# Splitting the transposed probabilities on GpSimd alone, and moving stores, loads and row sums in a hand-made order of attention heads

## The chip, the core and the metric

The kernel runs on one core of a Trainium2 chip. The core has five engines that run side by side, each through its own instructions in order: TensorE (PE in the profile; its weight loads are PEld), VectorE (DVE), ScalarE (ACT), GpSimd (POOL) and SyncE (SP), which here only starts transfers. Engines wait for each other through semaphores. The metric is the time of one execution on the device, in microseconds (us); lower is better.

## What is computed

The reference is a small decoder trunk on a sequence of 2048 tokens, width 1024, in float32: a Mamba-2 layer, then one layer of latent attention with 16 heads, then a last normalisation. Only the attention matters here. For each head, 128 queries at a time:

```python
s = s.astype(jnp.float32) * scale
mask = (q0 + local)[:, None] >= jnp.arange(kv_len)[None, :]
p = jax.nn.softmax(jnp.where(mask, s, -jnp.inf), axis=-1).astype(v.dtype)
outs.append(jnp.einsum('bhqk,bkhd->bqhd', p, v[:, :kv_len]))
```

The outputs of the heads are multiplied by a gate and by an output matrix and added to the residual.

## The kernel before

The program has three stages. The first (Mamba layer, projections, keys, values and queries written to DRAM) and the last (`back`: gate, output product, normalisation) are not touched. The middle stage, `attention` and its `heads`, is.

**Jobs.** `heads` works through 64 jobs `n`, one for each head `h` (16) and block `qb` of 512 queries (4 a head). Within a job, `j` counts four tiles of 128 queries, `c` counts blocks of 512 keys (`qb + 1` of them, the last cut to the causal width), and `k` counts tiles of 128 keys. Float32 accuracy is had from pairs of float16 numbers, a high and a low half, so every product is made two or three times.

**Steps.** Each step is a small function inside `heads` with a letter as its name:

- S, on TensorE: scores of one (j, c) into a PSUM bank (`mm3`, lines 279 to 281, three products, and the mask at line 1436).
- M, on VectorE: the negated maximum of each row of a bank (L1444). N, on VectorE: the row's shift from up to four maxima, with a constant added (L1449, or L1452 and L1453).
- E, on ScalarE: the exponential into a float32 tile `Pr` in SBUF, with the row's sum into `sum` (L1459). There are 20 `Pr` buffers. E gives the PSUM bank back.
- Key blocks other than c = 0, and all of `qb` 0, are turned on TensorE: T (L1481) transposes into PSUM, A on ScalarE (L1488) writes the high half and B on VectorE (L1493) the low half into `PTs`.
- The block c = 0 of the jobs with `qb` 1 to 3 (`TURNED`) is turned by DMA, 192 tiles in all: H on VectorE (L1465) casts `Pr` to float16, which is the high half in `HL`; L on GpSimd (L1469) subtracts it from `Pr`, which gives the low half and frees `Pr`; X on SyncE (L1475) starts a transposing DMA from `HL` to `PX`.
- V, on TensorE (L1507, L1508): the product with the values, `PTs` tiles first, `PX` tiles last in a job. F, on ScalarE (L1515): the job's output from PSUM to `Os`.
- O: two stores of `Os`. The first, on SyncE's queue (L1539), writes the product of the high halves of the values to `o_d` in DRAM. The second, on GpSimd's queue (L1540), adds the product of the low halves to the same place with an accumulating DMA, and so waits at GpSimd until the first has landed.
- R, on VectorE, once a head: row sums (L1520), reciprocal (L1521), a constant factor (L1522). Y, on TensorE (L1526), transposes them; Z (L1531, L1532) stores them.

**The order.** The stage is scheduled by hand. The class `Pace` plays the jobs through before the program is built: it books each step for a stated number of nanoseconds on its engine, with a stated delay until the next step may start, and appends the step to one list. The steps are then emitted in that list's order, and each engine runs its own in that order, however late the one at its head is. `queue(engine, rank, ...)` makes a step wait in the model until its engine is free; a lower rank goes first. A step that uses several engines, as O does, is appended once.

**Loads.** Queries, keys and values of the next head are loaded by SyncE. They are issued inside S of a job's first score (`load_q`, L1389 to L1391; for `qb` 2 also `load_k`, L1376 and L1377, and `load_v`, L1383), and the model of the order does not book them. The store O is appended when F ends in the model, without a booking either.

Of the kernel before, what the change touches and what calls it, by code (L numbers as in the profile page):

```python
# [15 lines left out]
AF = mybir.ActivationFunctionType  # L16
ALU = mybir.AluOpType
AX = mybir.AxisListType
# [3 lines left out]
P = 128  # L22
T = 2048
D = 1024
DI = 2048
G = 4
H = 32
NH = 16
EPS = 1e-6
TB = 512  # L30
NB = T // TB
# [16 lines left out]
def DVE(n):  # L48
    return 62 + n * 1.042, 135
KV2, CQ2, GA2, ALL2 = 0, 576, 1344, 3392  # L50
MAGIC = 12582912.0
PSCALE = 32768.0
PSHIFT = 10.397207708399179
# [18 lines left out]
class Pace:  # L72
# [79 lines left out]
    def scores(self, n, j, c):  # L152
        w, qb = self.width(n, j, c), self.jobs[n][1]
        self.give(ps=-1)
        self.scored += 1

        def maximum():
            self.issue("DVE", ("M", n, j, c), *DVE(w), after=counted)

        def counted():  # L160
            self.maxima[n, j] = self.maxima.get((n, j), 0) + 1
            if self.maxima[n, j] == qb + 1:
                self.queue("DVE", 1, lambda: self.issue("DVE", ("N", n, j), 100 if qb < 2 else 180, 110, shift))

        def shift():
            for x in range(qb + 1):
                self.queue("ACT", 2, lambda x=x: self.exp(n, j, x), lambda: self.free["Pr"] > 0)

        self.issue("PE", ("S", n, j, c), 3 * (w / 2.4 + 2.5) + 60 * (c == qb), 225,
                   lambda: self.queue("DVE", 2, maximum))  # L170

    def exp(self, n, j, c):
        w = self.width(n, j, c)
        self.give(Pr=-1)

        def done():
            self.give(ps=1)
            self.scored -= 1
            if (j, c) == (3, NB - 1):
                self.queue("DVE", 3, lambda: self.issue("DVE", ("R", n), 600, 130, summed))  # L180
            if c in self.turned[self.jobs[n][1]]:
                self.queue("DVE", 3, lambda: self.high(n, j, c),
                           lambda: self.free["HL"] > 0 and ((n, c) in self.dma or self.free["PX"] > 0))
            else:
                self.probs[n, j, c] = w // P

        def summed():
            self.sums.append(n)

        self.issue("ACT", ("E", n, j, c), 300 + w * 0.7, 40, done)  # L190

    def high(self, n, j, c):
        self.give(HL=-1, PX=-((n, c) not in self.dma))
        self.dma.setdefault((n, c), 4)

        def low():
            self.issue("POOL", ("L", n, j, c), 1364, 60, moved)

        def moved():
            self.give(Pr=1)  # L200
            self.queue("SP", 1, lambda: self.issue("SP", ("X", n, j, c), 1300, DMA_DELAY, landed))

        def landed():
            self.give(HL=1)
            self.dma[n, c] -= 1
            if not self.dma[n, c]:
                for k in range(4 * c, 4 * c + 4):
                    self.pairs[n, k] = "PX"

        self.issue("DVE", ("H", n, j, c), 345, 130, lambda: self.queue("POOL", 1, low))  # L210

    def rows(self, n):
        self.give(ps=-1)
# [24 lines left out]
    def values(self, n, k):  # L238
        w, qb = (4 - self.first(n, k)) * P, self.jobs[n][1]
        if n not in self.opened:  # L240
            self.opened[n] = 4 * qb + 4
            self.give(ps=-1)
        self.opened[n] -= 1
        last = not self.opened[n]

        def done():
            if self.pairs[n, k] == "PTs":
                self.give(PTs=1)
            else:
                c = k // 4  # L250
                self.dma[n, c] -= 1
                self.give(PX=self.dma[n, c] == -4)
            if last:
                self.queue("ACT", 0, lambda: self.issue("ACT", ("F", n), 495, 110, closed))

        def closed():
            self.order.append(("O", n))
            self.give(ps=1)

        self.issue("PE", ("V", n, k), 2 * (w / 2.4 + 2.5), 225, done)  # L260


class Net:
# [42 lines left out]
    def split(self, hi, lo, src, scale=None):  # L306
        nc = self.nc
        if scale is None:
            nc.scalar.activation(hi, src, AF.Copy)  # L309
            nc.vector.tensor_tensor(lo, src, hi.bitcast(F32), ALU.subtract)  # L310
        else:
            nc.scalar.activation(hi, src, AF.Copy, scale=scale)
            nc.vector.scalar_tensor_tensor(lo, src, scale, hi.bitcast(F32), ALU.mult, ALU.subtract)
# [1093 lines left out]
    def heads(self, sp):  # L1407
        nc, v = self.nc, self.nc.vector
        keys, vals, quer = self.keys, self.vals, self.quer
        pace = Pace(TURNED)  # L1410
        jobs = pace.jobs
        used = {"mm": 0, "tr": 0}
        sums, shifts, maxima, banks, probs, turned, halves, moved, outs = ({} for _ in range(9))

        def bank(first):
            tag = first if used[first] < 4 else "tr" if first == "mm" else "mm"
            used[tag] += 1
            return self.t(self.pp, tag, [P, TB], bufs=4), tag

        def S(n, j, c):  # L1420
            h, qb = jobs[n]
            if j == c == 0:
                if qb == 0:
                    sums[h] = self.t(sp, "sum", [P, 16, 4], bufs=3)
                    nc.gpsimd.memset(sums[h], 0.0)
                if h + 1 < NH:
                    if qb == 2:
                        self.load_k(h + 1, 0, NB, nc.sync)
                        self.load_v(h + 1, nc.sync)
                    self.load_q(h + 1, qb, nc.sync)  # L1430
            Q, K, w = quer[h, qb], keys[h], pace.width(n, j, c)
            s, tag = bank("mm")
            qs, ks = slice(j * P, (j + 1) * P), slice(c * TB, c * TB + w)
            self.mm3(s[:, :w], Q[:, 0, qs], Q[:, 1, qs], K[:, 0, ks], K[:, 1, ks], True, c < qb)
            if c == qb:
                nc.tensor.matmul(s[:, w - P:w], self.idb, self.mk, start=False, stop=True)
            if c == 0:
                shifts[n, j] = self.t(sp, "nm", [P, 1], bufs=4)
                maxima[n, j] = self.t(sp, "mx", [P, 4], bufs=4)
            banks[n, j, c] = s, tag, w  # L1440

        def M(n, j, c):
            s, _, w = banks[n, j, c]
            v.tensor_reduce(maxima[n, j][:, c:c + 1], s[:, :w], AX.X, ALU.max, negate=True)  # L1444

        def N(n, j):
            qb, m, nm = jobs[n][1], maxima.pop((n, j)), shifts[n, j]
            if qb == 1:
                v.tensor_scalar(nm, m[:, 0:1], m[:, 1:2], PSHIFT, ALU.min, ALU.add)  # L1449
                return  # L1450
            if qb:
                v.tensor_reduce(nm, m[:, :qb + 1], AX.X, ALU.min)  # L1452
            v.tensor_scalar(nm, nm if qb else m[:, 0:1], PSHIFT, None, ALU.add)  # L1453

        def E(n, j, c):
            h, qb = jobs[n]
# [3 lines left out]
                                 accum_out=sums[h][:, 4 * qb + j, c:c + 1])  # L1460
            used[tag] -= 1

        def H(n, j, c):
            u = halves[n, j, c] = self.t(sp, "HL", [P, 2, TB], F16, bufs=BUFS["HL"])
            v.tensor_copy(u[:, 0], probs[n, j, c])  # L1465

        def L(n, j, c):
            u = halves[n, j, c]
            nc.gpsimd.tensor_tensor(u[:, 1], probs.pop((n, j, c)), u[:, 0], ALU.subtract)  # L1469

        def X(n, j, c):
            if (n, c) not in moved:
# [38 lines left out]
        def F(n):  # L1511
            h, qb = jobs[n]
            o, tag, _ = outs[n]
            u = outs[n] = self.t(sp, "Os", [P, TB], bufs=3)
            nc.scalar.activation(u, o, AF.Copy)  # L1515
            used[tag] -= 1

        def R(n):
            ri = outs["ri"] = self.t(sp, "ri", [P, 16], bufs=2)
            v.tensor_reduce(ri, sums[jobs[n][0]], AX.X, ALU.add)  # L1520
            v.reciprocal(ri, ri)  # L1521
            v.tensor_scalar(ri, ri, 0.5 * PSCALE, None, ALU.mult)  # L1522

        def Y(n):
            outs["ps"] = bank("tr")
# [2 lines left out]
        def Z(n):  # L1528
            ps, tag = outs["ps"]
            r = self.t(sp, "rT", [16, P], bufs=2)  # L1530
            nc.scalar.activation(r, ps[:16, 0:P], AF.Copy)  # L1531
            nc.sync.dma_start(self.ri_d[jobs[n][0]].rearrange("(j q) -> j q", q=P), r)  # L1532
            used[tag] -= 1

        def O(n):
            h, qb = jobs[n]
            o = outs.pop(n)
            od = self.o_d[h * 64:(h + 1) * 64, qb * TB:(qb + 1) * TB]
            nc.sync.dma_start(od, o[0:64, :])  # L1539
            nc.gpsimd.dma_start(od, o[64:128, :], accum_op=ALU.add)  # L1540
            if h == NH - 3:
                self.load_wo(qb)

        steps = dict(S=S, M=M, N=N, E=E, H=H, L=L, X=X, T=T, A=A, B=B, V=V, F=F, O=O, R=R, Y=Y, Z=Z)
        for what, *where in pace.run():
            steps[what](*where)

# [197 lines left out]
```

## Time and profile before

| | us |
|---|---|
| median of 3 runs | 3231.45 |
| lowest and highest run | 3227.48, 3243.19 |
| profiled execution, its own time | 3242.9 |
| its span, first to last instruction | 3241.0 |
| attention stage in it (from the first score to the last output) | 2062 to 3055, 993 long |

A page of the profile gives, for each engine, the time in which it was busy and its share of the span; then the span in 40 slices, with the TensorE clock that was granted in tenths of full speed; then groups of instructions with their mean durations. Other views of the same trace answer questions for a stretch of time: who waited for whom, the instructions in order of time, and the busy time of each engine by window. Times within the trace are microseconds from the span's start. A wait is put down to the instruction that released it last, so an instruction just behind the true cause can stand there.

### The profile page before, as it was taken

Reading aid. Unit: us, or ns where it says so; the run is one execution under the profiler, and the core shown is the slowest. Engines: PE = TensorE matmul, PEld = TensorE weight load, DVE = VectorE, ACT = ScalarE, POOL = GpSimd, SP = SyncE. Lnnn points to the kernel's source line nnn. Section 1 sums busy time; section 2 is a strip of 40 time slices with the busy share of each in tenths; the row PEclk is TensorE's granted clock in tenths of the full one; section 3 lists DMA queues with packets and bytes.
Section 4 is the critical chain, followed back from the end, with each engine's and each line's share of the span. In section 5 each row is a group of like instructions: output and inputs, shape, how many; then the busy total and the mean of one; then the engine's idle time right before and its main releaser. Section 6 shows DMA issues by size and latency. Waiting matters only on the chain. (4 is left out here: it accounts for less than half of the span.)

```text
span 3241.0 us, 49983 instructions
## 1 busy us (share of the span) xinstructions
PE 3004.5 (93%) x17047; PEld 1876.4 (58%) x17047; DVE 2324.8 (72%) x4739; ACT 1882.4 (58%) x4760; POOL 699.0 (22%) x822
## 2 busy tenths in 40 slices
PE   8999999999999999999999999988888988887898
PEld 6777655555655556555655545455544554544687
DVE  6878887787777777877654454677877776888665
ACT  7878566666565565655434333566666666666422
POOL 1222112211212112112121122322322222224200
PEclk9999999999999999999999999999989999998999
DMA  5443666555554356544376566564565565565585
GB/s 174 130 127 122 203 225 223 187 179 172 196 184 147 114 178 223 182 146 149 120 252 205 162 195 189 138 113 88 104 118 93 98 121 95 95 131 125 116 269 173
DMA packets 456371, 507.11 MB, mean 156 GB/s; under 512 B 262626, under 2 KB 316130, under 8 KB 454676
## 3 DMA queue, kind: packets, MB, share of 16 engines
q1 hardware_dynamic: 439012, 457.37, 50.7%
q0 software_dynamic: 17104, 46.55, 5.2%
q8 instruction: 135, 2.21, 0.3%
q14 instruction: 120, 0.98, 0.1%
HBM read 332.21 MB, written 121.25 MB: 140 GB/s over the span
## 5 line engine op out<-in xcount | busy, mean ns | idle before, releaser
L1459 ACT ACTIVATE Pr<-mm,nm 128x512 f32<-128x512 f32 (+3 forms) x522 | 324.0, 629 | 95.2 <-POOL HL L1469 61.5
L1444 DVE TENSOR_REDUCE mx<-mm 128x1 f32<-128x512 f32 (+3 forms) x522 | 308.4, 602 | 72.7 <-PE mm L281 50.0
L1493 DVE TENSOR_TENSOR PTs<-tr,PTs 128x512 f16<-128x512 f32 (+2 forms) x447 | 251.8, 570 | 113.6 <-ACT PTs L1488 110.2
L279 PE MATMUL mm<-xT,wsp 128*128 128x512 f16 (+1 forms) x800 | 308.7, 386 | 0.8 <-ACT wsp L309 0.8
L280 PE MATMUL mm<-xT,wsp 128*128 128x512 f16 (+1 forms) x800 | 306.3, 383 | 0.0
L1469 POOL TENSOR_TENSOR HL<-Pr,HL 128x512 f16<-128x512 f32 x192 | 236.0, 1368 | 320.6 <-ACT Os L1515 123.3
L281 PE MATMUL mm<-xT,wsp 128*128 128x512 f16 (+1 forms) x800 | 304.6, 383 | 0.3 <-DVE wsp L310 0.2
L1488 ACT ACTIVATE PTs<-tr 128x512 f16<-128x512 f32 (+2 forms) x447 | 221.1, 509 | 139.1 <-PE tr L1481 136.8
L1481 PE MATMUL tr<-pack,Pr 128*128 128x128 f32 x1407 | 235.2, 288 | 32.7 <-ACT Pr L1459 16.7
L279 PE MATMUL mm<-K,xT 96*128 96x512 f16 (+4 forms) x530 | 192.8, 364 | 69.0 <-ACT Pr L1459 67.8
L279 PE MATMUL mm<-wsp,xT 128*128 128x512 f16 (+2 forms) x640 | 234.0, 367 | 4.4 <-ACT craw L877 3.0
L883 DVE SCALAR_TENSOR_TENSOR cacc<-craw,pack,cacc 128x512 f32<-128x512 f32 x288 | 217.1, 773 | 28.4 <-ACT cacc L881 26.6
L280 PEld LDWEIGHTS <-xT 128*128 128x128 f16 (+1 forms) x1280 | 127.4, 100 | 187.1 <-issue 101.9
L280 PE MATMUL mm<-wsp,xT 128*128 128x512 f16 (+2 forms) x640 | 233.2, 365 | 1.4 <-DVE wsp L318 1.3
L1481 PEld LDWEIGHTS tr<-pack,Pr 128*128 128x128 f32 x1407 | 178.9, 149 | 95.3 <-DVE PTs L1493 22.5
L281 PE MATMUL mm<-wsp,xT 128*128 128x512 f16 (+2 forms) x640 | 233.0, 365 | 0.0
L1036 POOL TENSOR_TENSOR Xp<-Xw,Xp 128x512 fp32r<-128x512 f32 x64 | 86.7, 1355 | 610.3 <-ACT Xp L1035 592.4
L279 PE MATMUL mm<-wsp,yT 128*128 128x512 f32 x512 | 210.2, 411 | 3.1 <-DMA wsp<-wo_d 2.0
L280 PE MATMUL mm<-wsp,yT 128*128 128x512 f32 x512 | 204.3, 399 | 0.0
L281 PE MATMUL mm<-wsp,yT 128*128 128x512 f32 x512 | 203.7, 399 | 0.0
L281 PEld LDWEIGHTS <-xT 128*128 128x128 f16 (+1 forms) x1280 | 126.5, 99 | 123.6 <-issue 12.7
L1064 ACT ACTIVATE big<-big,d_cum 128x128 f32<-128x128 f32 x512 | 168.1, 391 | 48.7 <-DMA big<-cumT 48.6
(462 smaller groups left out, 7561.1 us busy)
## 6 DMA issues: line engine op xcount, KB each, us to landing
wsp<-wo_d SPq DMA_DIRECT2D x96, 512.0 KB, 3.9
wsp<-w_d SPq DMA_DIRECT2D x68, 512.0 KB, 4.4
wraw<-in_ssm_w_in_dram SPq DMA_DIRECT2D x128, 256.0 KB, 3.2
big<-cumT SPq DMA_DIRECT2D x64, 512.0 KB, 5.0
wo_d<-wsp SPq DMA_DIRECT2D x32, 512.0 KB, 3.4
w_d<-wsp SPq DMA_DIRECT2D x32, 512.0 KB, 3.6
st<-w_d SPq DMA_DIRECT2D x56, 256.0 KB, 2.9
wsp<-wu_d SPq DMA_DIRECT2D x28, 512.0 KB, 3.8
```

The lines of the kernel that those rows point to most:

```text
L279: mm(out, l_hi, r_hi, start=start, stop=False)
L280: mm(out, l_hi, r_lo, start=False, stop=False)
L281: mm(out, l_lo, r_hi, start=False, stop=stop)
L883: nc.vector.scalar_tensor_tensor(acc, raw[:, k:k + TB], wk[k], acc, ALU.mult, ALU.add)
L1036: nc.gpsimd.tensor_tensor(u[:, 1], x, u[:, 0].bitcast(F32), ALU.subtract)
L1064: act(E[:, h, :], E[:, h, :], AF.Relu, bias=ncum[:, h0 + h:h0 + h + 1])
L1444: v.tensor_reduce(maxima[n, j][:, c:c + 1], s[:, :w], AX.X, ALU.max, negate=True)
L1459: nc.scalar.activation(x[:, :w], s[:, :w], AF.Exp, bias=shifts[n, j], accum_out=sums[h][:, 4 * qb + j, c:c + 1])
L1469: nc.gpsimd.tensor_tensor(u[:, 1], probs.pop((n, j, c)), u[:, 0], ALU.subtract)
L1481: nc.tensor.transpose(pt[:, j * P:(j + 1) * P], probs[n, j, k // 4][:, k % 4 * P:(k % 4 + 1) * P], self.ident)
L1488: nc.scalar.activation(u[:, 0, c], pt[:, c], AF.Copy)
L1493: v.tensor_tensor(u[:, 1, c], pt[:, c], u[:, 0, c], ALU.subtract)
```

## The change

- H is gone. L now makes both halves on GpSimd, a copy and a subtraction, and the model books 2200 ns on GpSimd for the pair, where it booked 345 on VectorE and 1364 on GpSimd.
- N uses reductions only. The maxima lie in a ring of six tiles of six columns, whose last column is set to the constant once; the smallest maximum goes to the column beside it, and the two are added by a reduction.
- R loses its constant factor, which moves into the scale of Z's activation. The model books 450 ns for R and 2000 ns until Y may follow (before: 600 and 130).
- The loads become a step D of their own, queued at SyncE with rank 2 (behind O, rank 0, and X, rank 1) and booked with 3500 or 1800 ns.
- O becomes two steps. The store on SyncE is queued with rank 0 and booked with 600 ns; the accumulating store on GpSimd, now G, is queued with rank 0 not earlier than 6000 ns after it, and booked with 900 ns.
- `Os` has four buffers, where it had three.

```diff
+        if j == c == 0:
+            self.queue("SP", 2, lambda: self.issue("SP", ("D", n), 3500 if qb == 2 else 1800))
...
-                self.queue("DVE", 1, lambda: self.issue("DVE", ("N", n, j), 100 if qb < 2 else 180, 110, shift))
+                self.queue("DVE", 1, lambda: self.issue("DVE", ("N", n, j), 200 if qb else 100, 110, shift))
...
-                self.queue("DVE", 3, lambda: self.issue("DVE", ("R", n), 600, 130, summed))
+                self.queue("DVE", 3, lambda: self.issue("DVE", ("R", n), 450, 2000, summed))
             if c in self.turned[self.jobs[n][1]]:
-                self.queue("DVE", 3, lambda: self.high(n, j, c),
+                self.queue("POOL", 1, lambda: self.split(n, j, c),
                            lambda: self.free["HL"] > 0 and ((n, c) in self.dma or self.free["PX"] > 0))
...
-            self.issue("POOL", ("L", n, j, c), 1364, 60, moved)
...
-        self.issue("DVE", ("H", n, j, c), 345, 130, lambda: self.queue("POOL", 1, low))
+        self.issue("POOL", ("L", n, j, c), 2200, 60, moved)
...
         def closed():
-            self.order.append(("O", n))
             self.give(ps=1)
+            self.queue("SP", 0, lambda: self.issue("SP", ("O", n), 600, 6000, lambda: self.queue(
+                "POOL", 0, lambda: self.issue("POOL", ("G", n), 900))))
...
+        ring = [self.t(sp, f"mx{i}", [P, 6], bufs=1) for i in range(6)]
+        for m in ring:
+            v.memset(m[:, 5:6], PSHIFT)
...
         def M(n, j, c):
             s, _, w = banks[n, j, c]
-            v.tensor_reduce(maxima[n, j][:, c:c + 1], s[:, :w], AX.X, ALU.max, negate=True)
+            at = c if jobs[n][1] else 4
+            v.tensor_reduce(maxima[n, j][:, at:at + 1], s[:, :w], AX.X, ALU.max, negate=True)
 
         def N(n, j):
-            qb, m, nm = jobs[n][1], maxima.pop((n, j)), shifts[n, j]
-            if qb == 1:
-                v.tensor_scalar(nm, m[:, 0:1], m[:, 1:2], PSHIFT, ALU.min, ALU.add)
-                return
+            qb, m = jobs[n][1], maxima.pop((n, j))
             if qb:
-                v.tensor_reduce(nm, m[:, :qb + 1], AX.X, ALU.min)
-            v.tensor_scalar(nm, nm if qb else m[:, 0:1], PSHIFT, None, ALU.add)
+                v.tensor_reduce(m[:, 4:5], m[:, :qb + 1], AX.X, ALU.min)
+            v.tensor_reduce(shifts[n, j], m[:, 4:6], AX.X, ALU.add)
...
-        def H(n, j, c):
+        def L(n, j, c):
+            x = probs.pop((n, j, c))
             u = halves[n, j, c] = self.t(sp, "HL", [P, 2, TB], F16, bufs=BUFS["HL"])
-            v.tensor_copy(u[:, 0], probs[n, j, c])
-
-        def L(n, j, c):
-            u = halves[n, j, c]
-            nc.gpsimd.tensor_tensor(u[:, 1], probs.pop((n, j, c)), u[:, 0], ALU.subtract)
+            nc.gpsimd.tensor_copy(u[:, 0], x)
+            nc.gpsimd.tensor_tensor(u[:, 1], x, u[:, 0], ALU.subtract)
...
-            v.tensor_scalar(ri, ri, 0.5 * PSCALE, None, ALU.mult)
...
-            nc.scalar.activation(r, ps[:16, 0:P], AF.Copy)
+            nc.scalar.activation(r, ps[:16, 0:P], AF.Copy, scale=0.5 * PSCALE)
```

D holds the loads that stood in S, unchanged. O and G hold the two stores that stood in O:

```python
        def O(n):
            h, qb = jobs[n]
            nc.sync.dma_start(self.o_d[h * 64:(h + 1) * 64, qb * TB:(qb + 1) * TB], outs[n][0:64, :])
            if h == NH - 3:
                self.load_wo(qb)

        def G(n):
            h, qb = jobs[n]
            nc.gpsimd.dma_start(self.o_d[h * 64:(h + 1) * 64, qb * TB:(qb + 1) * TB], outs.pop(n)[64:128, :],
                                accum_op=ALU.add)
```

More of the change, by code (lines that the diff above doesn't have):

```diff
@@ L190, in exp, with split @@
         self.issue("ACT", ("E", n, j, c), 300 + w * 0.7, 40, done)
-    def high(self, n, j, c):
+    def split(self, n, j, c):
         self.give(HL=-1, PX=-((n, c) not in self.dma))
         self.dma.setdefault((n, c), 4)
-        def low():
-            self.issue("POOL", ("L", n, j, c), 1364, 60, moved)
         def moved():
@@ L1425, in S @@
                     nc.gpsimd.memset(sums[h], 0.0)
[L1426 to L1430, printed above, removed]
             Q, K, w = quer[h, qb], keys[h], pace.width(n, j, c)
@@ L1438, in S, with D @@
                 shifts[n, j] = self.t(sp, "nm", [P, 1], bufs=4)
-                maxima[n, j] = self.t(sp, "mx", [P, 4], bufs=4)
+                maxima[n, j] = ring[(4 * n + j) % len(ring)]
             banks[n, j, c] = s, tag, w
+        def D(n):
+            h, qb = jobs[n]
+            if h + 1 < NH:
+                if qb == 2:
+                    self.load_k(h + 1, 0, NB, nc.sync)
+                    self.load_v(h + 1, nc.sync)
+                self.load_q(h + 1, qb, nc.sync)
         def M(n, j, c):
             s, _, w = banks[n, j, c]
-            v.tensor_reduce(maxima[n, j][:, c:c + 1], s[:, :w], AX.X, ALU.max, negate=True)
+            at = c if jobs[n][1] else 4
+            v.tensor_reduce(maxima[n, j][:, at:at + 1], s[:, :w], AX.X, ALU.max, negate=True)
         def N(n, j):
-            qb, m, nm = jobs[n][1], maxima.pop((n, j)), shifts[n, j]
-            if qb == 1:
-                v.tensor_scalar(nm, m[:, 0:1], m[:, 1:2], PSHIFT, ALU.min, ALU.add)
-                return
+            qb, m = jobs[n][1], maxima.pop((n, j))
             if qb:
-                v.tensor_reduce(nm, m[:, :qb + 1], AX.X, ALU.min)
-            v.tensor_scalar(nm, nm if qb else m[:, 0:1], PSHIFT, None, ALU.add)
+                v.tensor_reduce(m[:, 4:5], m[:, :qb + 1], AX.X, ALU.min)
+            v.tensor_reduce(shifts[n, j], m[:, 4:6], AX.X, ALU.add)
         def E(n, j, c):
@@ L1513, in F @@
             o, tag, _ = outs[n]
-            u = outs[n] = self.t(sp, "Os", [P, TB], bufs=3)
+            u = outs[n] = self.t(sp, "Os", [P, TB], bufs=4)
             nc.scalar.activation(u, o, AF.Copy)
@@ L1536, in O @@
             h, qb = jobs[n]
[L1537 to L1540, printed above, removed]
+            nc.sync.dma_start(self.o_d[h * 64:(h + 1) * 64, qb * TB:(qb + 1) * TB], outs[n][0:64, :])
             if h == NH - 3:
                 self.load_wo(qb)
-        steps = dict(S=S, M=M, N=N, E=E, H=H, L=L, X=X, T=T, A=A, B=B, V=V, F=F, O=O, R=R, Y=Y, Z=Z)
+        def G(n):
+            h, qb = jobs[n]
+            nc.gpsimd.dma_start(self.o_d[h * 64:(h + 1) * 64, qb * TB:(qb + 1) * TB], outs.pop(n)[64:128, :],
+                                accum_op=ALU.add)
+        steps = dict(S=S, M=M, N=N, E=E, D=D, G=G, L=L, X=X, T=T, A=A, B=B, V=V, F=F, O=O, R=R, Y=Y, Z=Z)
         for what, *where in pace.run():
```

## The prediction, made before the changed kernel was run

> **What bounds the kernel now.** I read the page first, then the busy time by windows, then, inside the stage that the change touches, who waited for whom, and last two of those waits instruction by instruction.
>
> ```profile
> span 3241.0 us, 49983 instructions
> PEclk9999999999999999999999999999989999998999
> ```
>
> ```profile
> core 0: us, PE busy (x) PEld busy (x) DVE busy (x) ACT busy (x) POOL busy (x), PEclk, DMA share, GB/s
> 2062.00:3055.00 993.00, 836.90 (x4888) 499.67 (x4887) 774.36 (x1719) 645.91 (x1818) 296.19 (x280) 0.93 0.57 105
> 0.00:2062.00 2062.00, 1992.89 (x11411) 1235.69 (x11412) 1435.52 (x2791) 1196.17 (x2868) 402.01 (x541) 1.00 0.54 175
> 3055.00:3241.00 186.00, 174.68 (x751) 141.00 (x749) 114.92 (x230) 40.36 (x74) 0.83 (x1) 0.97 0.74 221
> ```
>
> TensorE bounds every stage, but only attention gives it long rests: it stands idle there for 993 - 836.9 = 156 us, and its clock is 0.93 against 1.00 in the stage before. The other two stages (2248 us) stay as they are.
>
> ```profile
> PE mm L279 <- ACT Pr L1459: 67.8, 56, 8.7
> PE tr L1526 <- DVE nm L1453: 53.2, 14, 12.7
> PE tr L1481 <- ACT Pr L1459: 16.7, 7, 4.0
> PE tr L1481 <- DVE PTs L1493: 15.5, 16, 4.6
> ```
>
> These four rows (us in total, times, longest) are 153 of the 156 us. No row names `PX`: products with the DMA-turned tiles never came too early. The second row is the clearest case:
>
> ```profile
> 2409.52 0.83 POOL L1540 DMA_DIRECT2D o_d<-Os  x1 [3.13 <-ACT Pr L1459]
> 2409.90 3.88 DVE L1522 TENSOR_SCALAR ri<-ri 128x16 f32<-128x16 f32 x1
> 2410.12 3.62 POOL L1469 TENSOR_TENSOR HL<-Pr,HL 128x512 f16<-128x512 f32 x3
> 2413.93 0.37 PE L1526 MATMUL tr<-pack,ri 128*16 128x128 f32 x1 [3.95 <-DVE nm L1453]
> ```
>
> R's factor, 16 numbers a row, begins while GpSimd is at its store and ends only when GpSimd's burst ends. Y stands at the head of TensorE's order and waits, with everything behind it. The tiles' minimum, median and longest show which VectorE operations suffer so:
>
> ```profile
> L1465 DVE CAST HL<-Pr x192: 408/419/5926, 2068.0 to 3035.5; 128x512 f16<-128x512 f32 x192
> L1522 DVE TENSOR_SCALAR ri<-ri x16: 160/1292/4866, 2109.0 to 3040.3; 128x16 f32<-128x16 f32 x16
> L1493 DVE TENSOR_TENSOR PTs<-tr,PTs x447: 271/678/694, 2070.0 to 3049.2; 128x512 f16<-128x512 f32 x86, 128x128 f16<-128x128 f32 x21, 128x256 f16<-128x256 f32 x21, 128x384 f16<-128x384 f32 x21
> L1453 DVE TENSOR_SCALAR nm<-nm x128: 144/153/155, 2075.2 to 3028.6; 128x1 f32<-128x1 f32 x128
> ```
>
> H's cast and R's factor stretch up to fourteen- and thirtyfold; B (L1493) and N (L1453) never do. The first row of waits has another origin:
>
> ```profile
> 2360.26 4.33 SPq L1389 DMA_DIRECT2D xT<-qn_d  x1
> 2365.97 0.54 SPq L1539 DMA_DIRECT2D o_d<-Os  x1
> 2369.25 0.83 POOL L1540 DMA_DIRECT2D o_d<-Os  x1 [8.77 <-DMA o_d<-Os]
> 2369.83 3.65 POOL L1469 TENSOR_TENSOR HL<-Pr,HL 128x512 f16<-128x512 f32 x3
> 2371.30 0.69 ACT L1459 ACTIVATE Pr<-mm,nm 128x512 f32<-128x512 f32 x1 [9.51 <-POOL HL L1469]
> ```
>
> SyncE holds a load for 4.33 us, because the buffer is still in use; O's store behind it starts at 2365.97; the accumulating store waits for its landing at the head of GpSimd's order, and the splits behind it wait too. They hold `Pr` buffers, so the next exponential starts 9.51 us late, the PSUM banks stay full, and TensorE has no bank for scores. How often that happens:
>
> ```profile
> POOL o_d L1540 <- DMA o_d<-Os: 132.4, 29, 8.8
> ACT Pr L1459 <- POOL HL L1469: 90.3, 36, 9.5
> ```
>
> A rest also costs clock. After the 2.5 us rest before 2535.4 the next 5.6 us ran at 0.50, with TensorE busy throughout; stretches without a rest have 1.00:
>
> ```profile
> 2532.80:2535.40 2.60, 0.12 (x2) 0.08 (x2) 2.60 (x3) 0.04 (x1) 2.37 (x3) 0.88 0.84 154
> 2535.40:2541.00 5.60, 5.60 (x22) 3.37 (x23) 3.73 (x10) 3.45 (x11) 0.00 (x0) 0.50 0.68 142
> 2312.00:2344.00 32.00, 29.93 (x187) 18.12 (x186) 24.63 (x59) 23.91 (x69) 6.62 (x7) 1.00 0.35 65
> 2434.00:2466.00 32.00, 30.21 (x189) 18.34 (x187) 26.02 (x60) 24.16 (x69) 6.63 (x7) 1.00 0.35 65
> 2192.00:2220.00 28.00, 26.41 (x165) 16.18 (x164) 23.12 (x53) 20.28 (x58) 6.52 (x7) 1.00 0.25 46
> ```
>
> **The change, part by part.** The gain is not in the operations that go, since VectorE and GpSimd have idle time (774 and 296 busy of 993 us); it is in the rests of TensorE that they cause.
>
> *R without its factor, and Y booked 2 us later.* The factor is what Y waited for; the remaining two operations of R have no such stretch in the case shown (they end between 2409.37 and 2409.90). The 53.2 us go. Y's later place costs nothing while scores and products fill TensorE; at the very end of the stage it could cost 2 us, once.
>
> *H to GpSimd.* VectorE loses its stretched casts, and with them most of the 15.5 us in which a transpose waited for B. GpSimd gains 192 copies, an operation on a tile of this size that the trace does not have. The nearest rows:
>
> ```profile
> L1469 POOL TENSOR_TENSOR HL<-Pr,HL 128x512 f16<-128x512 f32 x192 | 236.0, 1368 | 320.6 <-ACT Os L1515 123.3 <-ACT PTs L1488 76.7 <-DVE nm L1452 58.5
> L1036 POOL TENSOR_TENSOR Ct<-BC,Ct 128x128 fp32r<-128x128 f32 x60 | 38.9, 648 | 119.6 <-ACT Ct L1035 119.6
> L876 POOL COPY craw<-halo 128x3 f32<-128x3 f32 x96 | 55.2, 576 | 170.4 <-DVE cacc L883 151.8 <-ACT wsp L309 5.9 <-DVE rm L393 3.5
> ```
>
> A copy of three numbers took 0.58 us, a subtraction of two tiles of the right size 1.37; between them, 384 more numbers cost a subtraction 0.72 us. A copy reads half as much, so I take the middle, 0.95 us: 192 x 0.95 = 182 us more on GpSimd (111 at the lower bound, 263 at the upper). GpSimd then has 296 + 182 = 478 us of work in a stage of some 850, so it does not become the bound in total. A job's four splits last 4 x 2.32 = 9.3 us instead of 5.5, and their `Pr` buffers come back that much later. The cover is the ring of 20: 640 exponentials (16 heads of 40) in 993 us are one per 1.55 us, so a buffer is wanted again after some 31 us, and after 26 in a stage of 850. I take 0 on the path; without cover it is the 182 us.
>
> *N by reductions.* The first two of these rows set its cost:
>
> ```profile
> L1452 DVE TENSOR_REDUCE nm<-mx 128x1 f32<-128x3 f32 x64 | 9.6, 150 | 0.7
> L1449 DVE TENSOR_SCALAR nm<-mx 128x1 f32<-128x1 f32 x64 | 13.0, 203 | 0.4
> L1465 DVE CAST HL<-Pr 128x512 f16<-128x512 f32 x192 | 107.8, 598 | 17.0 <-DMA PX<-HL 15.3 <-issue 1.5
> ```
>
> A small reduction takes 0.15 us, a one-column factor 0.15 (L1453): equal for `qb` 0, 2 and 3. For `qb` 1, 0.20 becomes 0.30, 64 times: 6 us of VectorE, against the 108 us that 192 casts took (median 0.42), so hidden. N's one-column operations never stretched, so N gains nothing either; bounds 0 and 6 us.
>
> *O, G and D.* The store goes ahead of the queued X and D, and G stands in GpSimd's order 6 us behind it instead of at once. What eats that margin is the wait inside a load, which the model does not book:
>
> ```profile
> L1389 SPq DMA_DIRECT2D xT<-qn_d x58: 538/582/4517, 2063.3 to 2933.2; - x58
> o_d<-Os SPq DMA_DIRECT2D x64, 128.0 KB, 2.4
> ```
>
> 6.0 less 2.4 to land leaves 3.6 us; the worst load takes 4.52 instead of 0.58, so 3.9 more. The margin just about holds, and most of the 67.8 + 16.7 us go. D moves three loads a job (six with keys and values) past X and O; they are wanted a head later, 62 us (993 / 16), so 0. X behind a late D waits as before. The fourth `Os` buffer covers the 6 us in which G holds one.
>
> *The sum.* TensorE's own work at full clock: the granted deficit is 0.07 x 993 = 70 us, of which some fell into the rests; I take 60 (bounds 40 and 70). 836.9 - 60 = 777 us. In the three stretches without a long rest TensorE was busy 86.55 of 92 us, 0.941. So 777 / 0.941 = 826 us (767 if every small rest went too, 852 with 40 and the worst stretch's 0.935). What stays, first:
>
> ```profile
> L310 DVE TENSOR_TENSOR xT<-xT,xT x2: 3826/5418/7011, 2971.0 to 2995.2; 128x512 fp32r<-128x512 f32 x2
> ```
>
> Two operations of the last stage, run early in the last head, are stretched as well and are not touched: 10.8 us, taken as 10. For margins missed at O and G I take 12. The stage is 848 us, 145 less. Against the profiled execution: 3242.9 - 145 = 3097.9. That execution lies 11.5 above the median, so against the median 3231.45 - 145 = 3086.
>
> [...]
>
> **The rivals.**
>
> *GpSimd still stops for the store.* If loads and X hold SyncE back more than the 3.6 us of margin in half the jobs, half of 67.8 + 16.7 stays (42 us), with its part of the clock, 60 x 42 / 153 = 16: the gain is 87, the time 3144. For it: the load's wait is not booked. Against: it was over by 2364.6 in the case shown, and the store is now ahead of the X's.
>
> *The clock stays low.* If it follows the stage and not the rests, 60 / 0.941 = 64 us of the gain are missing: 3150. Against: 1.00 in all three calm stretches.
>
> *VectorE waits for GpSimd in its other operations.* With bursts 1.7 times as long, what casts suffered might pass to B: the casts' mean of 0.60 less their median of 0.42 is 0.18 us, 448 times, 80 us: 3166. Against: B's longest was 0.694 beside a median of 0.678, through every burst so far.
>
> [...]
>
> *Slower: the exponentials wait for `Pr`.* If the ring does not cover the longer splits, ScalarE waits 0.95 us for each of 192, the PSUM banks stay full as in the chain above, and 182 us stand against 145: 3086 + 182 = 3268, and 3349 at 1.37 us a copy. It decides from 145 / 192 = 0.76 us uncovered per split. For it: the 90.3 us are just this wait. Against: 36 times in 640, and in the case shown behind a late store, not for want of speed.
>
> **How the numbers follow.** The forecast has 0.72; its own range is 3040 to 3115. GpSimd still stopping 0.12, the low clock 0.04, VectorE's other waits 0.03, the slower case 0.05, no change because several of these meet 0.02; still faster than 3040 (the 767 us stage) 0.02. The range 3040 to 3150 takes in the first two rivals. About half a per cent, 16 us, is what a measurement of this kernel can tell: faster 0.93, same 0.02, slower 0.05.
>
> **What would show it.** Right: no wait of Y's transpose over 1 us; VectorE without operations of several us before 2900; GpSimd at its second store waiting under 30 us in total for the first; the stage near 850 us with a clock over 0.97. Wrong: GpSimd busy over 600 us, rows in which exponentials wait over 60 us for L, products that wait for `PX`, or a clock that stays at 0.93 while the rests are gone.

## The result and the profile after

The changed kernel takes 3092.26 us (median of 4 runs, 3088.74 to 3094.81) against 3235.77 for the kernel before in the same comparison: a ratio of 0.9556, 95% interval 0.9528 to 0.9585. The profiled execution took 3091.5 us. Its page, with the lines shown of before:

```profile
span 3089.6 us, 49799 instructions
PEclk9999999999999999999999999999999999999999
```

The busy time of each engine in the attention stage, which now runs from 2053 to 2904, and in the stage before it (columns as before: length, busy times, clock, share of the DMA engines):

```profile
2053.00:2904.00 851.00, 797.30 (x4894) 481.47 (x4893) 644.66 (x1582) 636.51 (x1819) 409.44 (x473) 0.99 0.69 124
0.00:2053.00 2053.00, 1987.90 (x11398) 1234.13 (x11399) 1437.76 (x2790) 1195.38 (x2867) 402.03 (x540) 1.00 0.54 175
```

The stage is 142 us shorter (993 to 851). The other 9 us of the two profiles' difference lie in the first stage, which is the same code in both. TensorE now rests 851 - 797 = 54 us instead of 156, and its clock is 0.99 instead of 0.93. What it and GpSimd wait for in the stage:

```profile
PE mm L279 <- ACT Pr L1464: 35.9, 78, 2.5
PE tr L1510 <- DVE PTs L1496: 7.2, 12, 0.6
PE tr L1484 <- DVE PTs L1496: 5.8, 2, 5.4
```

```profile
POOL HL L1471 <- ACT Pr L1464: 197.5, 71, 9.8
POOL o_d L1545 <- DMA o_d<-Os: 142.7, 34, 7.2
```

Three things are to be seen. No wait of Y's transpose is left, and the scores' waits are many and short. GpSimd still stands for 143 us at its second store, waiting for the first to land: more than before (132). But no exponential waits for GpSimd's splits any more; L does not occur among ScalarE's waits. The two instructions of the new split, with minimum, median and longest duration:

```profile
L1471 POOL CAST HL<-Pr x192: 599/609/1072, 2060.5 to 2889.9; 128x512 f16<-128x512 f32 x192
L1472 POOL TENSOR_TENSOR HL<-Pr,HL x192: 1146/1155/1427, 2061.2 to 2890.6; 128x512 f16<-128x512 f32 x192
```

The number was forecast well (3086). That GpSimd still waits for the store, and TensorE does not care, does not fit the forecast's account of the gain. The experiments take that account apart.

### The profile page after: what moved, and what is told of

Same layout as the page of the kernel before. It is cut to its first block, busy times and chain, and to the rows that moved or that the text cites. A ratio compares the mean times of both kernels' runs of the same rounds, so it can differ in the third digit from the quotient of the medians.

```text
span 3089.6 us, 49799 instructions
## 1 busy us (share of the span) xinstructions
PE 2960.0 (96%) x17047; PEld 1856.9 (60%) x17047; DVE 2197.4 (71%) x4601; ACT 1872.3 (61%) x4760; POOL 812.3 (26%) x1014
## 4 chain that ended last, share of the span: by engine, by line
PE 57%; issue 11%; ACT 11%; DVE 11%; DMA 6%; POOL 3%; SPq 1%; ACTq 0%; POOLq 0%; DVEq 0%
PE mm L279 12%; PE mm L281 12%; PE mm L280 12%; PE tr L1484 4%; ACT Pr L1464 3%; PE tr L1510 3%; PE tr L1511 3%; DVE cacc L883 2%; PE tr L279 2%; PE tr L281 2%; PE tr L280 2%; DMA wraw<-in_ssm_w_in_dram 2%; ACT PTs L1491 2%; PE tr L1087 1%; ACT Xw L1080 1%
## 5 line engine op out<-in xcount | busy, mean ns | idle before, releaser
L1452 DVE TENSOR_REDUCE mx<-mm 128x1 f32<-128x512 f32 (+3 forms) x529 | 316.9, 614 | 136.6 <-PE mm L281 100.8
L1464 ACT ACTIVATE Pr<-mm,nm 128x512 f32<-128x512 f32 (+3 forms) x529 | 332.5, 641 | 54.4 <-DVE nm L1458 37.9
L279 PE MATMUL mm<-xT,wsp 128*128 128x512 f16 (+1 forms) x800 | 308.7, 386 | 0.0
L1491 ACT ACTIVATE PTs<-tr 128x512 f16<-128x512 f32 x448 | 219.6, 512 | 131.1 <-PE tr L1484 129.6
L1496 DVE TENSOR_TENSOR PTs<-tr,PTs 128x512 f16<-128x512 f32 x448 | 249.0, 570 | 45.4 <-ACT PTs L1491 41.5
L279 PE MATMUL mm<-wsp,xT 128*128 128x512 f16 (+2 forms) x640 | 233.1, 366 | 3.5 <-ACT craw L877 2.3
L1472 POOL TENSOR_TENSOR HL<-Pr,HL 128x512 f16<-128x512 f32 x192 | 222.1, 1157 | 15.4
L279 PE MATMUL mm<-K,xT 96*128 96x512 f16 (+4 forms) x537 | 189.5, 353 | 37.2 <-ACT Pr L1464 35.9
L1484 PE MATMUL tr<-pack,Pr 128*128 128x128 f32 x1408 | 212.4, 275 | 7.4 <-DVE PTs L1496 5.8
L279 PE MATMUL mm<-wsp,yT 128*128 128x512 f32 x512 | 210.0, 411 | 3.3 <-DMA wsp<-wo_d 2.2
L1484 PEld LDWEIGHTS tr<-pack,Pr 128*128 128x128 f32 x1408 | 168.9, 142 | 63.5 <-ACT Os L1518 8.2
```

What stands on the lines that cost most here:

```text
L279: mm(out, l_hi, r_hi, start=start, stop=False)
L1452: v.tensor_reduce(maxima[n, j][:, at:at + 1], s[:, :w], AX.X, ALU.max, negate=True)
L1464: nc.scalar.activation(x[:, :w], s[:, :w], AF.Exp, bias=shifts[n, j], accum_out=sums[h][:, 4 * qb + j, c:c + 1])
L1472: nc.gpsimd.tensor_tensor(u[:, 1], x, u[:, 0], ALU.subtract)
L1484: nc.tensor.transpose(pt[:, j * P:(j + 1) * P], probs[n, j, k // 4][:, k % 4 * P:(k % 4 + 1) * P], self.ident)
L1491: nc.scalar.activation(u[:, 0, c], pt[:, c], AF.Copy)
```

## The experiments

All times are medians beside runs of the kernel before on the same chip: 3228.99 us for `engine_only`, `order_only`, `cast_back` and `factor_back`; 3229.11 for `no_factor_only`, `split_only`, `store_at_once` and `loads_in_S`; 3235.15 for the other four. Behind each time stands its ratio to the kernel before, with the 95% interval. Many edits also let the model of the order make another list of steps; such a run measures the edit and the new order together.

### The engine edits alone, and the order alone

The first kernel takes the new split, N and R (and the four `Os` buffers), and keeps the order's rules of before. The second takes the new order and keeps H, N and the factor on VectorE.

```diff
 # engine_only, against the changed kernel
-            self.queue("SP", 2, lambda: self.issue("SP", ("D", n), 3500 if qb == 2 else 1800))
-            self.queue("SP", 0, lambda: self.issue("SP", ("O", n), 600, 6000,
...
+            self.order.append(("O", n)); self.order.append(("G", n))
-   self.issue("DVE", ("R", n), 450, 2000, summed)
+   self.issue("DVE", ("R", n), 450, 130, summed)
 # and the loads inside S again
```

> The new split on GpSimd, N by reductions and R without its factor, but the order as before: loads inside S, both stores appended when F ends, Y booked 130 ns behind R. Theory A (blocked VectorE operations cost the time): Y's 53 us and the 16 us of waits for B go, with their part of the clock, about 95 us: some 3140 us. Theory B (the late store and its place in the order cost it): no more than 55 us of gain, 3180 us or above, with TensorE's waits for exponentials still 60 us or more.

Measured: 3112.09 us, 0.9633 (0.9607 to 0.9659), 117 us less than before.

```diff
 # order_only, against the changed kernel
-            nc.gpsimd.tensor_copy(u[:, 0], x)
+            v.tensor_copy(u[:, 0], probs[n, j, c])        # as a step H, booked 345 as before
+            v.tensor_scalar(ri, ri, 0.5 * PSCALE, None, ALU.mult)
-   self.issue("DVE", ("R", n), 450, 2000, summed)
+   self.issue("DVE", ("R", n), 600, 2000, summed)
 # and N as before
```

> The new order (loads as a step of SyncE, G 6 us behind O, Y 2 us behind R, four Os buffers), but H's cast, N and R's factor on VectorE as before. Theory A: the blocked casts and the factor still stop TensorE, 3150 us or above, with casts of several us in the trace. Theory B: 84 us of waits and 33 us of clock go: about 3120 us or below.

Measured: 3167.99 us, 0.9822 (0.9792 to 0.9851), 61 us less. Theory A comes nearer in both runs. But each half brings something, the engine edits more than theory A gave them, and 117 + 61 is more than the 143 of the whole: in part they remove the same rests.

### The cast back on VectorE, and the factor back

Two kernels with all of the change but one edit.

```diff
 # cast_back
-            nc.gpsimd.tensor_copy(u[:, 0], x)
+            v.tensor_copy(u[:, 0], probs[n, j, c])        # as a step H, booked 345 as before
```

> The changed kernel with H's cast on VectorE again, all else as changed. Theory A: casts of several us come back behind GpSimd's bursts and stores, TensorE waits 20 to 40 us more: 3115 to 3140 us. Theory B: the order hides it, within 10 us of the changed kernel (3092).

Measured: 3176.18 us, 0.9831 (0.9814 to 0.9849), some 84 us more than the changed kernel. With H on VectorE the model also makes another order. The group of casts in it, TensorE's two largest waits, and the stretch from 2200 to 2880, which is steady in all three kernels, for the kernel before, the changed one and this one:

```profile
L1471 DVE CAST HL<-Pr 128x512 f16<-128x512 f32 x192 | 151.4, 833 | 4.7 <-DMA PX<-HL 2.8 <-issue 1.6 <-ACT Pr L1465 0.3
```

```profile
PE mm L280 <- ACT Pr L1465: 56.3, 78, 4.6
PE tr L1487 <- DVE PTs L1499: 35.1, 16, 2.4
```

```profile
2200.00:2880.00 680.00, 575.10 (x3370) 344.05 (x3369) 518.99 (x1182) 439.41 (x1249) 190.75 (x187) 0.93 0.57 103
```

```profile
2200.00:2880.00 680.00, 636.96 (x3931) 385.64 (x3930) 518.78 (x1270) 510.66 (x1467) 325.91 (x377) 0.99 0.70 127
```

```profile
2200.00:2880.00 680.00, 599.01 (x3589) 357.77 (x3588) 572.65 (x1298) 465.29 (x1332) 213.63 (x198) 0.97 0.63 113
```

A cast takes 0.41 us at the shortest and 0.83 on average here, and VectorE is busy 573 of 680 us (84%) for less of the work: 3589 instructions on TensorE against 3931. Transposes now wait for B (L1499), 35.1 us where it was 5.8. One such place, instructions in order of time (a row can hold several):

```profile
2306.64 3.34 DVE L1471 CAST HL<-Pr 128x512 f16<-128x512 f32 x4
2307.20 4.90 POOL L1475 TENSOR_TENSOR HL<-Pr,HL 128x512 f16<-128x512 f32 x4 [19.70 <-ACT Os L1521]
2309.90 0.88 DVE L1499 TENSOR_TENSOR PTs<-tr,PTs 128x384 f16<-128x384 f32 x2
2310.50 1.30 PE L1487 MATMUL tr<-pack,Pr 128*128 128x128 f32 x5 [2.44 <-DVE PTs L1499]
```

Two of the four casts take 0.42 us. The other two begin while a subtraction runs on GpSimd, end just behind it and take 1.38 and 1.37 us; the subtractions beside them take 1.20 to 1.33 us, where the changed kernel's have a median of 1.155. Two low halves (B) stand behind the casts on VectorE, and the next transposes stand behind those for 2.44 us. Casts last up to 2.56 us here and 5.93 before, where the longest runs from 2960.09 to 2966.02, and two GpSimd operations beside it from 2960.84 to 2965.72. M's reductions on VectorE, which run beside the same subtractions in the kernel before, take at most 0.69 us there and in the changed kernel. So casts were held beside GpSimd's operations in these runs, and M was not; what holds them is not shown.

```diff
 # factor_back
+            v.tensor_scalar(ri, ri, 0.5 * PSCALE, None, ALU.mult)
-            nc.scalar.activation(r, ps[:16, 0:P], AF.Copy, scale=0.5 * PSCALE)
+            nc.scalar.activation(r, ps[:16, 0:P], AF.Copy)
-   self.issue("DVE", ("R", n), 450, 2000, summed)
+   self.issue("DVE", ("R", n), 600, 2000, summed)
```

> The changed kernel with R's constant factor on VectorE again, all else as changed (Y still 2 us behind R). Theory A: the factor is held for 1 to 5 us in most of the 16 heads, and all of VectorE behind it; Y waits beyond its 2 us: 15 to 40 us more, 3107 to 3132 us. Theory B: the later Y hides it, within 8 us of 3092.

Measured: 3087.95 us, 0.9564 (0.9544 to 0.9584), the same as the changed kernel. R is booked with 600 ns again here, so the order is not quite the changed kernel's. The factor, which had a median of 1.29 us before, is hardly held:

```profile
L1525 DVE TENSOR_SCALAR ri<-ri x16: 174/174/2034, 2099.0 to 2888.5; 128x16 f32<-128x16 f32 x16
```

### One edit in the kernel before

If the factor is worth nothing at the end of the change, is it worth something at the start? And what does the cast bring alone?

```diff
 # no_factor_only, against the kernel before
-   self.issue("DVE", ("R", n), 600, 130, summed)
+   self.issue("DVE", ("R", n), 450, 130, summed)
-            v.tensor_scalar(ri, ri, 0.5 * PSCALE, None, ALU.mult)
-            nc.scalar.activation(r, ps[:16, 0:P], AF.Copy)
+            nc.scalar.activation(r, ps[:16, 0:P], AF.Copy, scale=0.5 * PSCALE)
```

> The kernel before with one edit: R's constant factor goes into the scale of Z's activation. Theory A (Y's 53 us of waits belong to the held factor, as the prediction's first term has it): those 53 us and some 20 us of clock go, 3229 - 73 = about 3156 us. Theory C (what is held behind GpSimd's burst is VectorE as such; the next cast is held in the factor's place): a gain under 25 us, 3205 us or above.

Measured: 3281.98 us, 1.0158 (1.0139 to 1.0176): 53 us slower than before, where both theories spoke of a gain (theory C's bound takes the time in, its reason does not). The edit had a second part, the booking of 600 ns cut to 450, and that alone lets the model make another order. The next kernel keeps the booking:

```diff
 # no_factor_same_order, against the kernel before: as above, R booked 600 as before
```

> The kernel before without R's factor on VectorE, as in the run with that one edit, but R stays booked with 600 ns, so that every engine runs in exactly the order of before. Theory E (in that run the shorter booking made another order, and the order cost the 51 us; the held factor itself is worth its 53 us of Y's waits and their clock): about 3160 us. Theory C (what is held passes to the next cast or exponential): within 25 us of before (3229) or slower.

Measured: 3229.0 us, 0.9977 (0.9966 to 0.9988): 6 us, not 73. Its waits in the stage (of TensorE, of GpSimd, of ScalarE):

```profile
PE mm L279 <- ACT Pr L1459: 75.5, 56, 8.3
PE tr L1481 <- ACT Pr L1459: 42.3, 7, 7.1
PE tr L1525 <- DVE nm L1453: 16.9, 7, 3.4
PE tr L1481 <- DVE PTs L1493: 16.3, 17, 4.6
```

```profile
POOL o_d L1539 <- DMA o_d<-Os: 176.6, 31, 8.4
```

```profile
ACT Pr L1459 <- POOL HL L1469: 126.4, 42, 9.1
```

Y's waits fell from 53.2 to 16.9 us, and the transposes' waits for exponentials rose from 16.7 to 42.3, the scores' from 67.8 to 75.5. The sum of the four rows is 151 us, where it was 153. TensorE arrives earlier and then waits longer for exponentials, and these wait longer for the splits (126.4 us instead of 90.3), which stand on GpSimd behind its store. Most of the rest was moved, not removed.

```diff
 # split_only, against the kernel before
-                self.queue("DVE", 3, lambda: self.high(n, j, c),
+                self.queue("POOL", 1, lambda: self.high(n, j, c),
-        self.issue("DVE", ("H", n, j, c), 345, 130, lambda: self.queue("POOL", 1, low))
+        self.issue("POOL", ("L", n, j, c), 2200, 60, moved)
...
-            v.tensor_copy(u[:, 0], probs[n, j, c])
+            nc.gpsimd.tensor_copy(u[:, 0], x)
```

> The kernel before with one edit: both halves are made on GpSimd (copy and subtraction, 2200 ns booked), R's factor stays on VectorE and the order's rules stay. Theory A: Y still waits for the held factor, now behind bursts of twice the length, 50 us or more: 3160 us or above. Theory C (the casts are what counts, and the factor was only in their company): within 15 us of the run with all the engine edits (3112).

Measured: 3095.52 us, 0.9583 (0.9566 to 0.9601). This one edit, with factor, N, loads and stores by the old rules, gives 134 of the 143 us, and its interval overlaps that of the whole change. It is 17 us faster than the run with all engine edits (3112), with the intervals apart: the other engine edits, with their bookings, took some of the gain back. Theory C's 15 us around 3112 are just missed, on the better side. The model makes another order here too, since the split is now booked on GpSimd alone. Waits of TensorE and GpSimd, and the factor's row:

```profile
PE mm L276 <- ACT Pr L1456: 42.5, 75, 5.0
```

```profile
POOL o_d L1535 <- DMA o_d<-Os: 47.7, 7, 17.4
```

```profile
L1517 DVE TENSOR_SCALAR ri<-ri x16: 174/208/618, 2101.3 to 2894.4; 128x16 f32<-128x16 f32 x16
```

### Stores and loads by the old rules in the changed kernel

```diff
 # store_at_once
-            self.queue("SP", 0, lambda: self.issue("SP", ("O", n), 600, 6000,
...
+            self.order.append(("O", n)); self.order.append(("G", n))
```

> The changed kernel with both stores appended at F's end again, as before; loads and Y in their new places. Prediction's step (the accumulating store that stops GpSimd's splits cost 67.8 + 16.7 us of waits): half of it or more comes back, 3130 us or above, with exponentials waiting for L. Theory D (the ring of 20 Pr buffers covers a stopped GpSimd once VectorE is free): within 12 us of 3092.

Measured: 3189.46 us, 0.9875 (0.9854 to 0.9895), some 100 us more than the changed kernel. Waits of TensorE, GpSimd and ScalarE:

```profile
PE mm L279 <- ACT Pr L1464: 106.6, 115, 5.8
```

```profile
POOL o_d L1545 <- DMA o_d<-Os: 335.8, 33, 17.1
```

```profile
ACT Pr L1464 <- POOL HL L1472: 83.9, 50, 6.0
```

With loads booked at SyncE and the stores not, GpSimd stops 33 times, for up to 17 us, the splits stand behind it, and exponentials wait 83.9 us for the ring of `Pr` buffers. So the chain from the store to TensorE is real. A single stop does not make it: the run with the split alone has one of 17.4 us too, stops for 47.7 us in all and gains 134. The run also shows that an edit of the order is not worth a fixed amount: the run with the engine edits alone appends its stores in the same way and takes 3112. The two differ in the loads' and Y's bookings; which of these makes the 77 us was not tried apart.

```diff
 # loads_in_S
-            self.queue("SP", 2, lambda: self.issue("SP", ("D", n), 3500 if qb == 2 else 1800))
+        # load_k, load_v and load_q inside S, as before
```

> The changed kernel with the loads inside S again; O, G and Y in their new places. Prediction's step (the load's unbooked wait holds up the store and X): 10 to 30 us more than 3092. Theory D: within 8 us of 3092.

Measured: 3090.46 us, 0.9571 (0.9549 to 0.9592): nothing.

### How fast GpSimd must be, and N

```diff
 # slow_split
+            nc.gpsimd.tensor_copy(u[:, 1], x)
             nc.gpsimd.tensor_copy(u[:, 0], x)
```

> The changed kernel with one more copy of the same tile on GpSimd in each of the 192 splits, not booked, so in the same order. It is overwritten by the subtraction. It measures whether the ring of 20 Pr buffers covers GpSimd's pace. Covered (the prediction's 0 on the path): within 12 us of 3092. Uncovered (the slower rival's mechanism): 0.64 us x 192 = 123 us more, 3200 us or above; half covered: about 3150.

Measured: 3093.64 us, 0.9566 (0.9551 to 0.9580). The added copies took their time (the row of the second copy; the window from 2200 to 2880, where GpSimd is busy 415 us instead of 326), and none of it reaches the end:

```profile
L1472 POOL CAST HL<-Pr x192: 606/616/1077, 2068.5 to 2897.3; 128x512 f16<-128x512 f32 x192
```

```profile
2200.00:2880.00 680.00, 636.47 (x3928) 385.14 (x3926) 518.38 (x1271) 510.65 (x1463) 414.99 (x535) 0.99 0.68 126
```

```diff
 # n_back
-            v.tensor_reduce(shifts[n, j], m[:, 4:6], AX.X, ALU.add)
+            v.tensor_scalar(nm, nm if qb else m[:, 0:1], PSHIFT, None, ALU.add)
 # and the other operations of N and M as before, same bookings
```

> The changed kernel with N's operations as before (one-column factors and additions on VectorE), same order. Prediction's step (N gains and costs nothing): within 8 us of 3092. If one-column operations were held behind GpSimd's longer bursts like the casts: 192 of them, some of over 1 us in the trace, 3110 us or above.

Measured: 3087.32 us, 0.9545 (0.9527 to 0.9563): N is worth nothing either way here, as forecast.

### An attempt at the rests that are left

```diff
-SCORED = 5
+SCORED = 6
```

> The changed kernel with six score banks allowed in flight in the order's model instead of five. What is left of TensorE's rests is scores that wait for a bank, 36 us in 78 short waits. If the limit of five causes them: 3060 to 3080 us. If the time from score to exponential does: within 8 us of 3092 or slower.

Measured: 3247.6 us, 1.0038 (1.0025 to 1.0051), slower than the kernel before by 0.4%. TensorE's largest waits and the window from 2200 to 2880:

```profile
PE tr L1484 <- DVE PTs L1496: 57.3, 76, 2.8
PE mm L279 <- ACT Pr L1464: 37.6, 57, 1.7
PE tr L279 <- ACT Pr L1464: 20.3, 30, 1.9
```

```profile
2200.00:2880.00 680.00, 574.99 (x3335) 321.30 (x3334) 453.54 (x1070) 436.11 (x1234) 268.26 (x317) 0.99 0.57 103
```

The scores' waits (the rows of L279, in both groups of banks) went from 36 to 58 us, so more banks for scores did not shorten them. And now transposes wait for B, 57 us where it was 5.8. Of the eight PSUM banks that the plan counts (`ps=8` in `BUFS`) six may hold scores, and two are left for transposes and outputs. The loss stands in the plan already: played through with its own bookings, the class `Pace` ends this stage at 953 us, where the changed kernel's ends at 797, and the measured loss is 155 us. Given a ninth bank, the model with six ends at 782, so in the plan it is the banks. No version beat the changed kernel clearly; the intervals of the three that lie a few us under it overlap its own.

## Why the prediction was right, and where its account was not

**The total.** The forecast was 145 us less than before; it was 143.5. That whole rests would go, with most of their clock, was right: TensorE rests 54 us instead of 156, at a clock of 0.99 instead of 0.93. The pace was right too: TensorE's share of the stage is 797.3 / 851 = 0.937, where 0.941 was taken. That the sum came so close is partly luck. TensorE's own work was put at 777 us and took 797 (the bound of 40 us for the clock would have given just this), and the 22 us added for what stays found nothing to stand for. The two errors cancel: 848 was forecast for the stage, and it takes 851.

**R's factor: the step that failed.** The prediction said that the 53.2 us of Y's waits go with the factor. Taken out alone in the same order it brought 6 us (0.9977), and put back at the end, with Y 2 us behind it, it costs nothing. The row "who waited" named what TensorE waited for there, not what the stage had to wait for: with Y released, the next transposes and scores waited instead.

**O and G: half right.** The chain from a late store to missing `Pr` buffers exists and can cost 100 us, as the run with the stores appended at once shows. But the prediction's sign of it, under 30 us of waits at GpSimd's second store, was wrong: they are 143 us, and no exponential waits for a split. The margin of 3.6 us by the bookings did not hold. What seems to matter is which splits stand behind G, and whether their buffers are wanted soon; that is read from these runs and was not tried apart.

**H: the term that was too small.** The prediction gave the casts little of their own (most of 15.5 us). Alone their move brings 134 us; back on VectorE they take 84. So the gain hangs on the step that the prediction counted least. Why it is worth so much is shown only in part. In the kernel before, being held lengthened the 192 casts by 34 us together (a mean of 0.598 us, a median of 0.419) and the subtractions by 41 (a mean of 1.368, now 1.157). The rest of the 134 is what stood behind them, or the other order: both runs moved the cast and changed the order. By its own bookings the model ends the stage at 774 us both before and with the split alone, and at 797 and 798 for the changed kernel and with the cast back, so neither plan is shorter. But a plan's length is not all: with R booked 450 ns it is 4 us longer and measured 59 us slower than with 600. A cast that is not held, in the order of before, would settle it; it was not tried.

**What was costed at nothing.** GpSimd's longer split: right, and with much to spare, as 0.62 us more in each of 192 splits cost nothing. So the slower rival fell: the ring covers GpSimd's pace, though not many long stops. N and the loads: right. The copy takes 0.61 us, not 0.95, and the pair 1.8 us, not 2.32 (the means in the stage are no longer than 0.64 and 1.16).

**What stays.** The two operations of the last stage that were expected to be held, 10.8 us before, took 0.69 us each this time. The longest rest left, 5.4 us at the end of the stage, has another cause: VectorE, which owes the transposes their B, stands 4.4 us at an operation of the last stage until a DMA load lands.

**The rivals.** The low clock fell (0.99). So did VectorE's other waits: B is not stretched beside the longer bursts.

```profile
L1496 DVE TENSOR_TENSOR PTs<-tr,PTs x448: 280/680/693, 2061.7 to 2900.1; 128x512 f16<-128x512 f32 x86, 128x128 f16<-128x128 f32 x23, 128x256 f16<-128x256 f32 x21, 128x384 f16<-128x384 f32 x20
```

GpSimd does stop for the store, as the first rival said, but without its price.

## What to carry to other kernels

When several engines wait in a ring, the rows of waits cannot be priced one by one: of 36 us of rest that left one row, 34 came back in other rows. The pace of a stretch without long rests was a good forecast of the stage here, once its long rests were gone. And where an order comes from a model with booked times, an edit's own worth is seen only with the order held: cutting one booking from 600 to 450 ns turned a gain of 6 us into a loss of 53.

## What the runs showed of the hardware that was not expected

The subtraction on GpSimd also gained from the casts' leaving VectorE, for the same tile. Its rows before (shown in the prediction, a mean of 1.368 us), in the changed kernel, and with the cast back on VectorE:

```profile
L1472 POOL TENSOR_TENSOR HL<-Pr,HL 128x512 f16<-128x512 f32 x192 | 222.1, 1157 | 15.4
```

```profile
L1475 POOL TENSOR_TENSOR HL<-Pr,HL x192: 1142/1321/1596, 2062.4 to 2975.2; 128x512 f16<-128x512 f32 x192
```

So in these runs the holding goes both ways: the subtraction has a median of 1.41 us before, 1.32 with the cast back, and 1.16 with no cast on VectorE.

What a rest cost in clock was not told by its length alone. In the run with six score banks TensorE is idle for 105 of the 680 us from 2200 to 2880, at a clock of 0.99; its three rows of waits above, which are those of the whole stage, have means of 0.75, 0.66 and 0.68 us. In the kernel before it is idle for the same 105 us, in 64 waits with a mean of 1.6 us and up to 8.7, at 0.93. But short rests did cost clock in places. In the run with six banks two rests of 0.98 and 0.92 us fall between 2560 and 2564, and the next 3 us run at half clock; its longest rest, of 2.8 us before 2972.94, is followed by half clock too. With the cast back, the rest of 2.44 us that is shown above has half clock behind it as well. The stretches, first of the run with six banks, then of the run with the cast back:

```profile
2560.00:2564.00 4.00, 2.09 (x11) 0.87 (x9) 1.38 (x2) 2.44 (x7) 0.00 (x0) 0.97 0.01 2
2564.00:2567.00 3.00, 3.00 (x9) 1.17 (x8) 1.38 (x2) 1.22 (x4) 1.76 (x2) 0.50 0.00 0
2975.00:2980.00 5.00, 4.88 (x16) 2.57 (x17) 2.40 (x6) 4.25 (x15) 5.00 (x4) 0.50 0.43 129
```

```profile
2310.50:2313.50 3.00, 3.00 (x10) 1.84 (x11) 1.25 (x3) 1.88 (x6) 2.37 (x3) 0.51 1.22 122
```

So rests of 2.4 to 2.8 us were enough in these places, and so were two of under 1 us each within 4 us. But other rests as long cost nothing: in the kernel before, one of 2.5 us that ends at 2781.74 has a clock of 1.00 in the 8.3 us behind it, and so has one of 2.9 us that ends at 2866.89, in 8.1 us. What decides between them is not shown here.
